# Other homes in SBUF for h^T, the slots and the table of constants of an encoder trunk kernel

## Chip, core and metric

The kernel runs on one core of a Trainium2 chip. The metric is the time of one execution on the device in microseconds, the median of several runs; lower is better.

## What is computed

Two layers of a bidirectional encoder trunk on 512 tokens of width 1024, all in float32. Each layer projects the normed input once (`w_in`, 1024 by 11,168 columns), feeds four token mixers and their gates from it, and merges the branches:

```python
for l in range(DEPTH):                       # 2
    h = rmsnorm(x, norm_pre[l])
    p = split_in(einsum("bsd,de->bse", h, w_in[l]))
    y_a = mixer_a(...) * silu(p["a_g"])      # dilated windows, 18 heads in 3 groups
    y_b = mixer_b(...) * silu(p["b_g"])      # conv and two linear recurrences
    y_c = mixer_c(...) * silu(p["c_g"])      # differential attention, 4 heads
    y_d = mixer_d(...) * silu(p["d_g"])      # latent attention, 6 heads
    g = sigmoid(p["gate"] + b_gate[l])       # 4 x 1024 gates
    merged = sum of g[i] * (y_i @ w_br_i[l]) over the four branches
    x = x + rmsnorm(merged @ w_out[l], norm_post[l])
```

## The kernel before

**Three products for one.** Every dense float32 product is made of three matmuls on operands of type float32r: a matrix is split into a high part (a copy rounded by ScalarE) and a low part (the rest, by VectorE), and `mm3` issues high by high, high by low and low by high into one PSUM bank. So weights come as pairs `wh`, `wl`, the normed and transposed input as `hTh`, `hTl`, a branch's output as `yb0h`, `yb0l` and so on, and the merged activations as `mh`, `ml`. Every matmul loads its stationary operand (128 by 128) anew.

**Which operand stands and which moves.** `item_T` computes 128 output channels at a time: the weights stand, and 512 tokens move, from `hTh`, `hTl` (projections, gates) or from a branch's output (`branch`). `item_tok` and `item_out` compute 128 tokens at a time: the activations stand (a 128-column block of `hTh`, `hTl`, `mh` or `ml`), and 512, 416 or 384 weight columns move. In the rows below the operand ahead of the comma moves and the one behind it stands; `ps<-hTh,wh` has h^T moving, `ps<-wh,hTh` has it standing.

**Where tiles live.** All SBUF is planned by hand. A pool of one-off tiles (`self.cp`) comes first, in `setup`; then 82 slots of 128 by 512 float32 (2048 bytes in each partition), from which nearly every work tile is taken by `slot`; then 4 staging tiles of the same size for raw weights, and small tiles. Tiles are laid one behind another in the order in which the code makes them, each start rounded up to 32 bytes. 1152 bytes of each partition are taken ahead of the first. h^T is two tiles of 8 blocks of 512 float32 (`hTh`, `hTl`, 16,384 bytes each). The table `cst` (9232 bytes: ALiBi distances, rotary tables) is read by VectorE and GpSimd; `junk` is where ScalarE leaves squares whose sums alone are wanted; `ident` is the identity for transposes.

**What sets the order.** A model of the five engines' times (`Sched`) decides, while the program is built, in which order the dense work (`dense_all`), the attention side work (`side_main`) and the recurrence (`side_lru`) are issued. It looks at sizes and tile names, not at addresses. All instructions are recorded from one helper line, L314.

Of the kernel before, what the change touches and what calls it, by code (L numbers as in the profile page):

```python
# [9 lines left out]
F32 = mybir.dt.float32  # L10
# [6 lines left out]
P = 128  # L17
# [17 lines left out]
K_C, K_A1, K_A23, K_RT, K_RN, K_QS, K_END = 0, 896, 1280, 1536, 2048, 2304, 2436  # L35
# [5 lines left out]

N_SLOT = 82
N_STAGE = 4
W_FIRST = 8
BANKS = {"d": 3, "S": 2, "T": 2, "O": 1}
W_MIN = 7
# [316 lines left out]
class Trunk:  # L363
# [131 lines left out]
    def load_w(self, upto):  # L495
        nc = self.nc
        while self.w_dma < min(upto, len(self.specs)):
            src, a, b = self.specs[self.w_dma]
            if self.w_dma < W_FIRST:
                st = self.slot("st")  # L500
            else:
                st = self.stp.tile([P, 512], F32, tag="st", name=self.uid("st"))
                self.clk.take(st, "st", N_STAGE)
            v = st[:, :a * b].rearrange("p (a b) -> p a b", a=a)
# [9 lines left out]
    def pump(self, force=None):  # L514
        cls, self.clk.cls = self.clk.cls, "w"
        self.load_w(max(W_FIRST, self.w_split) + N_STAGE)
        n = 0
        while self.w_split < self.w_dma:
# [10 lines left out]
            del self.stage[i]  # L529
            if i < W_FIRST:  # L530
                self.rel(st)
                if i == W_FIRST - 1:
                    self.done.add("first")
            self.w_split += 1
            n += 1
        self.load_w(max(W_FIRST, self.w_split) + N_STAGE)
        self.clk.cls = cls
# [442 lines left out]
    def side_first(self):  # L980
        V = self.nc.vector
        yield ("n", 2 + 8 + 4 + 8 + W_FIRST)

# [16 lines left out]
        xs.append(self.load_x(self.I["x"], 3))  # L1000
        self.load_w(W_FIRST + N_STAGE)
        self.nc.sync.dma_start(self.cst, self.I["consts"][:, P:])
# [705 lines left out]
    def setup(self):  # L1708
        nc, I = self.nc, self.I
        V, S = nc.vector, nc.scalar  # L1710
        self.cst = self.cp.tile([P, K_END - P], F32, name="cst")
        self.ident = self.cp.tile([P, P], F32, name="ident")
        self.junk = self.cp.tile([P, 512], F32, name="junk")
        self.tiny_t = self.cp.tile([P, 1], F32, name="tiny")
        nc.gpsimd.memset(self.tiny_t, 1.0e-30)
        self.tiny = self.tiny_t[:, 0:1]
        self.eps_t = self.cp.tile([P, 1], F32, name="eps")
        nc.gpsimd.memset(self.eps_t, EPS)
        self.eps = self.eps_t[:, 0:1]
        self.hTh = self.cp.tile([P, 8, 512], F32R, name="hTh")  # L1720
        self.hTl = self.cp.tile([P, 8, 512], F32R, name="hTl")
        self.prm = self.cp.tile([P, 256], F32, name="prm")
        self.prm_h = self.cp.tile([P, P], F32, name="prmh")
        self.prm_d = self.cp.tile([P, 32], F32, name="prmd")
        self.clk.free_of_war = {self.junk.tensor.name}
        self.clk.by_block = {t.tensor.name for t in (self.hTh, self.hTl)}

# [97 lines left out]
    def run(self):  # L1825
# [6 lines left out]
        with tc.tile_pool(name="c", bufs=1) as self.cp, tc.tile_pool(name="s", bufs=N_SLOT) as self.sp, \  # L1832
                tc.tile_pool(name="st", bufs=N_STAGE) as self.stp, tc.tile_pool(name="sm", bufs=40) as self.smp, \
                tc.tile_pool(name="sw", bufs=6) as self.smw, \
# [147 lines left out]
```

## Time and profile before

| | us |
|---|---|
| median of 3 runs (1566.57 to 1566.65) | 1566.58 |
| the profiled execution | 1567.27 |
| its span, first to last instruction | 1565.5 |
| PE (TensorE matmuls) busy in it | 1550.1 (99%) |
| DVE (VectorE) busy | 882.7 (56%) |
| ACT (ScalarE) busy | 734.8 (47%) |
| granted TensorE clock, mean | 0.997 of full speed |

A PE that is busy 99% of the span says that a matmul is always under way, not that matmuls follow one another as fast as they could: they overlap, and the end of one is modelled. How fast they go is read from the starts of two matmuls in the timeline, or of the first and the last of a run, divided by the steps between them. This is called the pace below.

### The profile page before, as it was taken

The numbers are of one execution on the slowest core, as the hardware profiler recorded it, in microseconds if no ns is written. First come the engines' busy times: TensorE is split into PE (matmuls) and PEld (weight loads), VectorE is DVE, ScalarE is ACT, GpSimd is POOL, SyncE is SP. The second block draws the span as 40 slices with busy tenths as digits, with TensorE's granted clock in tenths as the row PEclk, the third lists the DMA queues.
The fourth block names the chain that finished last, engine by engine and source line by source line (L and its number), as shares of the span: only waits on it lengthen the run. The fifth ranks groups of instructions, "written<-read, shape, count | busy, mean of one in ns | idle before, by whom it ended". The sixth has DMA issues, their size and how long they took to land.

```text
span 1565.5 us, 21989 instructions
## 1 busy us (share of the span) xinstructions
PE 1550.1 (99%) x8024; PEld 1257.3 (80%) x8024; DVE 882.7 (56%) x1898; ACT 734.8 (47%) x1626; POOL 59.1 (4%) x254
## 2 busy tenths in 40 slices
PE   8999999999999999999999999999999999999998
PEld 7877888778787888888888878887787787788886
DVE  5698754446544453556657876544546445445553
ACT  5576653343444443443456765434435445334331
POOL 1300000000000100000010000000000001000000
PEclk9999999999999999999999999999999999999999
DMA  6422132223232333253252212232232223332521
GB/s 209 140 58 57 44 101 78 78 71 94 68 79 71 86 74 105 58 174 104 72 166 54 68 55 80 79 85 68 75 94 61 77 72 86 80 95 58 183 71 54
DMA packets 170884, 136.34 MB, mean 87 GB/s; under 512 B 25230, under 2 KB 158360, under 8 KB 170648
## 3 DMA queue, kind: packets, MB, share of 16 engines
q1 hardware_dynamic: 170776, 134.94, 31.1%
q8 instruction: 63, 1.03, 0.3%
q14 instruction: 45, 0.37, 0.1%
HBM read 129.45 MB, written 4.27 MB: 85 GB/s over the span
## 4 chain that ended last, share of the span: by engine, by line
PE 98%; DVE 1%; ACT 1%; DMA 0%; issue 0%; SPq 0%; DVEq 0%; ACTq 0%
PE ps L314 98%; DMA st<-in_w_in 0%; DVE rr L314 0%; SPq L314 0%; DVE hTl L314 0%; ACT hTh L314 0%; DVE rp L314 0%; ACT h L314 0%; DVE x L314 0%; ACT wh L314 0%; DVE wl L314 0%; ACT junk L314 0%; DVE h L314 0%; DVE xc L314 0%; DVE yb2l L314 0%
## 5 line engine op out<-in xcount | busy, mean ns | idle before, releaser
L314 PE MATMUL ps<-hTh,wh 128*128 128x512 f32 x1280 | 520.9, 407 | 0.7 <-DVE ud L314 0.7
L314 PE MATMUL ps<-hTh,wl 128*128 128x512 f32 x1280 | 505.8, 395 | 0.0
L314 PE MATMUL ps<-hTl,wh 128*128 128x512 f32 x1280 | 505.1, 395 | 0.0
L314 DVE TENSOR_TENSOR wl<-st,wh 128x512 fp32r<-128x512 f32 (+2 forms) x464 | 301.7, 666 | 278.5 <-ACT wh L314 276.9
L314 PEld LDWEIGHTS ps<-hTh,wh 128*128 128x128 f32 x1280 | 241.1, 188 | 65.8 <-issue 13.2
L314 PEld LDWEIGHTS ps<-hTh,wl 128*128 128x128 f32 x1280 | 240.9, 188 | 56.4
L314 ACT ACTIVATE wh<-st 128x512 fp32r<-128x512 f32 (+2 forms) x464 | 265.3, 606 | 43.9 <-DMA st<-in_w_in 37.4
L314 PEld LDWEIGHTS ps<-hTl,wh 128*128 128x128 f32 x1280 | 241.6, 189 | 49.2
L314 DVE CUSTOM_DVE_ANT_0 pC<-ps,cst 128x512 f32<-128x512 f32 x64 | 41.6, 688 | 83.4 <-PE ps L314 83.4
L314 PE MATMUL ps<-wh,hTh 128*128 128x416 f32 (+2 forms) x192 | 72.0, 375 | 0.7 <-ACT hTh L314 0.6
L314 PE MATMUL ps<-wl,hTh 128*128 128x416 f32 (+2 forms) x192 | 70.3, 366 | 1.5 <-DVE wl L314 1.5
L314 PE MATMUL ps<-wh,hTl 128*128 128x416 f32 (+2 forms) x192 | 70.3, 366 | 0.2
L314 ACT ACTIVATE pA<-pA,on 128x256 f32<-128x256 f32 x96 | 47.9, 501 | 38.4 <-DVE on L314 38.1
L314 ACT ACTIVATE pD<-ps,mx 128x512 f32<-128x512 f32 x48 | 32.9, 686 | 66.1 <-DVE mx L314 66.0
L314 ACT ACTIVATE pC<-pC,mx 128x512 f32<-128x512 f32 x64 | 45.8, 717 | 36.3 <-DVE mx L314 36.3
L314 DVE CUSTOM_DVE_ANT_0 pA<-ps,cst 128x256 f32<-128x256 f32 x96 | 36.0, 420 | 32.2 <-PE ps L314 32.2
L314 PE MATMUL ps<-wh,mh 128*128 128x512 f32 x128 | 50.0, 391 | 0.0
L314 PE MATMUL ps<-wh,ml 128*128 128x512 f32 x128 | 49.9, 390 | 0.0
L314 PE MATMUL ps<-wl,mh 128*128 128x512 f32 x128 | 49.9, 390 | 0.0
L314 ACT ACTIVATE wtC<-ps 128x512 f32<-128x512 f32 x32 | 19.0, 595 | 52.0 <-PE ps L314 52.0
L314 ACT ACTIVATE junk<-ps,rd 128x128 f32<-128x128 f32 x32 | 11.7, 365 | 65.1 <-DVE oC L314 64.4
L314 DVE TENSOR_REDUCE mx<-ps 128x1 f32<-128x512 f32 x48 | 32.7, 686 | 14.7 <-PE ps L314 14.5
(390 smaller groups left out, 2210.7 us busy)
## 6 DMA issues: line engine op xcount, KB each, us to landing
st<-in_w_in SPq DMA_DIRECT2D x216, 256.0 KB
st<-in_w_in SPq DMA_DIRECT2D x240, 128.0 KB
st<-in_w_out SPq DMA_DIRECT2D x32, 256.0 KB
x<-in_x SPq DMA_DIRECT2D x16, 256.0 KB
st<-in_w_br_c SPq DMA_DIRECT2D x16, 256.0 KB
x<-x SPq DMA_DIRECT2D x16, 256.0 KB
st<-in_w_in SPq DMA_DIRECT2D x16, 208.0 KB
st<-in_w_in SPq DMA_DIRECT2D x16, 192.0 KB
```

The costliest lines, as they stand in the source:

```text
L314: op.fn(*op.a, **op.k)
```

## The change

Nothing is computed otherwise: every engine gets the same instructions in the same order, with the same waits. Other is where tiles live. `ident`, the two one-column tiles and `prm_d` come first, and a pad of 48 float32; then h^T; then `junk`, `prm` and `prm_h`; then `cst` and a pad of 120 float32; then the slots. The pads are tiles that nothing reads or writes.

```diff
+PAD = (48, 120)
...
-        self.cst = self.cp.tile([P, K_END - P], F32, name="cst")
+
         self.ident = self.cp.tile([P, P], F32, name="ident")
-        self.junk = self.cp.tile([P, 512], F32, name="junk")
         self.tiny_t = self.cp.tile([P, 1], F32, name="tiny")
...
         self.eps = self.eps_t[:, 0:1]
+        self.prm_d = self.cp.tile([P, 32], F32, name="prmd")
+        self.cp.tile([P, PAD[0]], F32, name="pad0")
         self.hTh = self.cp.tile([P, 8, 512], F32R, name="hTh")
         self.hTl = self.cp.tile([P, 8, 512], F32R, name="hTl")
+        self.junk = self.cp.tile([P, 512], F32, name="junk")
         self.prm = self.cp.tile([P, 256], F32, name="prm")
         self.prm_h = self.cp.tile([P, P], F32, name="prmh")
-        self.prm_d = self.cp.tile([P, 32], F32, name="prmd")
+        self.cst = self.cp.tile([P, K_END - P], F32, name="cst")
+        self.cp.tile([P, PAD[1]], F32, name="pad1")
```

The homes that follow, in bytes from the start of a partition:

| tile | before | its remainder by 512 | now | its remainder by 512 |
|---|---|---|---|---|
| `hTh` (8 blocks of 2048) | 13024 | 224 | 2048 | 0 |
| `hTl` | 29408 | 224 | 18432 | 0 |
| the slots (82 of 2048), then 4 staging tiles | 47456 on | 352 | 48128 on | 0 |
| `ident` | 10400 | 160 | 1152 | 128 |
| `junk` | 10912 | 160 | 34816 | 0 |
| `cst` | 1152 | 128 | 38400 | 0 |

A matmul operand begins at its tile's start, or 512, 1024 or 1536 bytes behind it. So before, every operand out of h^T begins at remainder 224 by 512, and every other operand of a dense matmul at 352; now all of them at 0.

## Rows read from the trace of the kernel before

**Rows 1.** The page: busy time of engines and share of span.
```profile
PE 1550.1 (99%) x8024; PEld 1257.3 (80%) x8024; DVE 882.7 (56%) x1898; ACT 734.8 (47%) x1626; POOL 59.1 (4%) x254
```

**Rows 2.** The chain that ended last: its longest pieces; start us, us, what.
```profile
92.64 703.92 PE ps L314 x3683
...
959.24 599.30 PE ps L314 x3131
```

**Rows 3.** Groups of PE, by shape: names, shapes, xcount, busy us, mean ns.
```profile
L314 PE MATMUL ps<-hTh,wh 128*128 128x512 f32 x1280 | 520.9, 407 | 0.7 <-DVE ud L314 0.7
L314 PE MATMUL ps<-hTh,wl 128*128 128x512 f32 x1280 | 505.8, 395 | 0.0
L314 PE MATMUL ps<-hTl,wh 128*128 128x512 f32 x1280 | 505.1, 395 | 0.0
L314 PE MATMUL ps<-wh,mh 128*128 128x512 f32 x128 | 50.0, 391 | 0.0
...
L314 PE MATMUL ps<-wh,hTh 128*128 128x512 f32 x64 | 25.8, 402 | 0.0
L314 PE MATMUL ps<-wh,hTl 128*128 128x512 f32 x64 | 25.2, 394 | 0.0
L314 PE MATMUL ps<-wl,hTh 128*128 128x512 f32 x64 | 25.2, 394 | 0.0
```

**Rows 4.** Timeline of PE, layer 2, first and last of 144 h^T matmuls.
```profile
1372.00 0.39 PE L314 MATMUL ps<-hTh,wh 128*128 128x512 f32 x1
...
1405.36 0.40 PE L314 MATMUL ps<-hTh,wl 128*128 128x512 f32 x1
```

**Rows 5.** Timeline of PE, end of layer 1, first and last of 132 slot matmuls.
```profile
732.95 0.39 PE L314 MATMUL ps<-ya0h,wh 128*128 128x512 f32 x1
...
762.66 0.39 PE L314 MATMUL ps<-wh,ml 128*128 128x512 f32 x1
```

**Rows 6.** Timeline of PE, early in layer 1, first and last of 102 h^T matmuls.
```profile
36.97 0.40 PE L314 MATMUL ps<-hTh,wh 128*128 128x512 f32 x1
...
60.44 0.39 PE L314 MATMUL ps<-hTh,wl 128*128 128x512 f32 x1
```

**Rows 7.** Those three stretches: busy us of each engine (instructions), PE clock, DMA share, GB/s.
```profile
1371.99:1405.37 33.38, 33.38 (x145) 26.86 (x143) 11.31 (x21) 8.93 (x16) 0.00 (x0) 1.00 0.34 96
732.94:762.67 29.73, 29.73 (x133) 24.61 (x132) 18.91 (x38) 12.13 (x25) 0.00 (x0) 1.00 0.26 82
36.96:60.45 23.49, 23.49 (x103) 19.06 (x103) 12.04 (x26) 11.36 (x23) 15.35 (x59) 1.00 0.72 211
```

**Rows 8.** Timeline of PE, a short slot run of branch c, first and last of 24.
```profile
547.17 0.39 PE L314 MATMUL ps<-yc0h,wh 128*128 128x512 f32 x1
...
552.43 0.40 PE L314 MATMUL ps<-yc3h,wl 128*128 128x512 f32 x1
```

**Rows 9.** Timeline of PE, branch b, nine slot matmuls behind four transposes.
```profile
249.20 0.60 PE L314 MATMUL ps<-ident,pD 128*128 128x128 f32 x4
249.55 0.48 PE L314 MATMUL ps<-yb0h,wh 128*128 128x512 f32 x1
249.87 0.40 PE L314 MATMUL ps<-yb0l,wh 128*128 128x512 f32 x1
250.10 0.39 PE L314 MATMUL ps<-yb0h,wl 128*128 128x512 f32 x1
250.33 0.39 PE L314 MATMUL ps<-yb1h,wh 128*128 128x512 f32 x1
...
251.46 0.39 PE L314 MATMUL ps<-yb2h,wl 128*128 128x512 f32 x1
```

**Rows 10.** Timeline of PE, slot matmuls of 384 columns, six from 71.62 on, then h^T.
```profile
71.62 0.34 PE L314 MATMUL ps<-ukvh,cTh 128*128 128x384 f32 x1
...
72.66 0.40 PE L314 MATMUL ps<-hTh,wh 128*128 128x512 f32 x1
```

## The prediction

> **What bounds the kernel.** I read the page's busy times first: PE has 1550.1 us of the span, DVE 882.7, ACT 734.8 [rows 1]. The chain that ended last says that this is a bound and not only a long row of work: one of its pieces is 3683 PE instructions over 703.92 us and another 3131 over 599.30 us, without a step to any other engine [rows 2]. So the time is the number of matmuls times the pace at which they start, and what a change does to DVE, ACT or DMA counts only if it makes PE wait. Most matmuls are of one kind: 3840 with h^T moving and 512 columns, in three groups of 1280, and 192 with h^T standing [rows 3].
>
> Next I read the pace from the starts. In a run of 144 matmuls with h^T, the first starts at 1372.00 and the last at 1405.36 us: 33.36 us over 143 steps, 233.3 ns each [rows 4]. In a run of 132 that begins in branch a and ends in `w_out`, where both operands lie in slots, it is 29.71 us over 131 steps, 226.8 ns [rows 5]. The shape is the same (512 columns, 128 by 128 standing), and so is the granted clock, 1.00 [rows 7], which is the level of 2.4 GHz. The h^T run is 6.5 ns slower per matmul.
>
> Who is to blame? Not the neighbours: in the slower run DVE worked 11.31 of 33.38 us (34%) and ACT 8.93 (27%), in the faster one 18.91 of 29.73 (64%) and 12.13 (41%) [rows 7]. Not the DMA: in an early run of 102 h^T matmuls its share was 0.72 instead of 0.34, and the pace was 23.47 us over 101 steps, 232.4 ns [rows 6, 7]. Not a wait: each run is one unbroken PE sequence. What is left is where the operands lie. An h^T operand begins at remainder 224 by 512 bytes, a slot operand at 352; in rows 4 the two kinds meet in each matmul, in rows 5 both operands begin at 352. The change takes that difference away.
>
> A second thing in the pace concerns all of them. Six slot matmuls of 384 columns take 1.04 us, 173.3 ns each [rows 10]. Between 384 and 512 columns lie 226.8 - 173.3 = 53.5 ns, 0.418 ns per column; 512 columns are then 214.0 ns, and 12.8 ns per matmul are left that don't depend on its length. What these are the trace doesn't say.
>
> **The change part by part.** No instruction is removed, added or moved, and no queue gets other work. The two pads cost nothing: nothing touches them.
>
> *h^T against slots.* The upper end of the gain is the whole difference of the long runs, 6.5 ns [rows 4, 5]. But a slot run begins slowly too. Behind transposes, the steps from 249.87 to 250.33 are 230 ns each, and only then, from 250.33 to 251.46, does it go on at 226 ns [rows 9]; a run of 24 in branch c took 5.26 us over 23 steps, 228.7 ns [rows 8], 4.6 ns under the long h^T run. Much of the dense work is cut into shorter pieces than that by side work, so I take 4 ns for all 3840 + 192 matmuls [rows 3]: **4032 x 4.0 ns = 16.1 us**. The lower end is 1 ns (a third of the first steps' advantage, since at 230 ns they are some 3 ns under the h^T pace), 4 us; the upper one 6.5 ns, 26.2 us.
>
> *Slots against slots.* Their remainder goes from 352 to 0, but that of the one operand against the other stays 0. I take no gain. The bounds are all of the 12.8 ns that don't depend on the length, for 4032 h^T matmuls and the 1008 slot matmuls of 512 columns in the branch and output products (13 x 8 x 3 x 2 and 8 x 4 x 2 x 3 x 2, together 1008): 64.5 us; and on the other side what the second rival says.
>
> *The other matmuls.* 8024 [rows 1] less 4032 and 1008 leaves some 3000: transposes, attention products of 64 to 128 columns, and a few hundred of 384 or 416. No row has one of these kinds at two homes; I take nothing. As bounds serve the 6.5 ns per 512 columns of rows 4 and 5, that is 1.6 ns per 128 columns, either way: 4.8 us more or less.
>
> *`cst`, `junk`, `ident`, parameters.* Their readers and writers are DVE, ACT and GpSimd, which have 44% of the span and more to spare [rows 1]; PE covers what they might gain or lose. If that cover were gone, PE would show waits for them within these long chains, and it shows none [rows 2]. DMA lands in slots at other remainders; at a share of 0.26 to 0.72 in the stretches looked at [rows 7] it has room as well.
>
> *What is late next.* Nothing, at 16 us: PE stays the bound, with its weights split ahead of it as before.
>
> *The sum.* The profiled execution took 1567.27 us (span 1565.5), 0.69 above the median of 1566.58. 1567.27 - 16.1 = 1551.2; against the median, **1550.5 us**, 1.0% faster.
>
> **The rivals.** First, *the constant part goes too*. If some of the 12.8 ns is paid because operands begin in the middle of what the array fetches at a time, a start at 0 saves it for every matmul. For it speaks that the cost doesn't grow with the length; against it, that nothing in this trace begins at a rounder place than another and goes faster. In full this is 64.5 us on top of up to 26.2: 1566.6 - 90.7 = 1476; half of it on top of 16 gives 1518. The page "TensorE: Matmul & The Clock Gate" of the Trainium skill (Back-to-back issue gap) gives the columns over the clock and about 2.5 ns for the step between warm matmuls, about 216 ns for 512 columns; the settled slot run at 226.8 ns [rows 5] doesn't agree, and by that page an estimate of 11 ns per matmul, 55 us, could still go.
>
> Second, *the place itself is bad, and the difference is not what counts*. Say that a beginning at a multiple of 512 costs as much as h^T's 224 does now. Then the h^T matmuls keep their 233 ns, and the 1008 slot matmuls go from 226.8 to it: 6.5 us more, 1573.1 us. This rival decides against the change once the slot pairs lose more than the h^T ones gain: with h^T unchanged, 3.1 us more (0.2%, about what a measurement of this kernel can tell from no change) need 3.1 ns for each slot matmul; against a gain of 4 ns for h^T, they would have to lose 16 ns. For it speaks that every tile now begins at the same remainder by 1024, so whatever is decided by these address bits happens to all at once; against it, that slots already share one remainder and are the faster kind.
>
> Third, *the change does nothing to PE*: h^T is slower for another reason than its remainder, for instance because it lies low in the partition, and stays so. h^T remains the lowest large tile. Then the time is 1566.6, with 1563.5 to 1569.7 around it. The same page of the Trainium skill (Step-by-step: what each phase is for) says that the array reads moving and standing operands through two ports of their own, so that loading the next weights takes nothing from the running matmul. By that rule how two operands lie to each other could not matter, and the sum would be 0; the trace has two paces that neither clock nor neighbours explain [rows 4, 5, 7], which speaks against the rule as far as it goes.
>
> **How the numbers follow.** The forecast gets 0.47; its own range is 1540 to 1563 us (26.2 and 4 us of gain). The constant part, in full or in part, gets 0.22 (1476 to 1540). No effect gets 0.17, the bad place 0.14 (up to 1573 and beyond). Faster by over 0.2%: 0.47 + 0.22 = 0.69; within 0.2%: 0.17; slower: 0.14. The range takes in the forecast, most of the first rival and most of "no effect", and leaves out the slow rival and the very end of the first: 1480 to 1569.
>
> **What would show it.** Right: in the long run of rows 4, 143 steps in about 32.4 us (226.8 ns), the run of rows 5 still at 226 to 227 ns, the same instruction counts, PE still 98% of the chain. If the first rival holds, both runs come under 224 ns and the slot matmuls of 384 columns under 171. If the second, the run of rows 5 comes to 230 ns or more. If the third, rows 4 stay at 233. I am wrong altogether if the pace improves and the time doesn't: then PE would have to wait for `wl` or `wh`, and steps in the chain to DVE, ACT or DMA would show where.

## The result and the profile after

The changed kernel takes **1548.98 us** (median of 4 runs, 1548.64 to 1550.21) against 1566.62 us for the kernel before (4 runs, 1566.57 to 1567.01): a ratio of 0.9888, 95% interval 0.9871 to 0.9905, 17.6 us less. The prediction was 1550.5 us. The profiled execution took 1549.14 us with a span of 1547.4, 18.1 under the span before.

The page of the changed kernel, busy time of engines and the chain that ended last (to be read beside [rows 1]; the helper line is L315 here, as the edit added a line):

```profile
PE 1532.6 (99%) x8024; PEld 1254.7 (81%) x8024; DVE 882.4 (57%) x1898; ACT 735.3 (48%) x1626; POOL 61.0 (4%) x254
...
PE 96%; DVE 1%; ACT 1%; DMA 0%; issue 0%; SPq 0%; DVEq 0%; ACTq 0%
```

The same number of instructions on every engine; DVE, ACT and the weight loads are busy as long as before, within 3 us. PE alone lost 17.5 us, and is still 99% of the span. Its share of the chain is 96% instead of 98, so some steps to ACT and DVE are now on it where I had expected none; they don't show as lost time, since PE's idle time in the span was 15.4 us and is 14.8 (span less busy). Its groups, by shape (beside [rows 3]; the last column but one is the mean duration in ns, whose end is modelled):

```profile
L315 PE MATMUL ps<-hTh,wh 128*128 128x512 f32 x1280 | 515.8, 403 | 1.1 <-DVE ud L315 1.1
L315 PE MATMUL ps<-hTl,wh 128*128 128x512 f32 x1280 | 499.7, 390 | 0.0
L315 PE MATMUL ps<-hTh,wl 128*128 128x512 f32 x1280 | 499.5, 390 | 0.0
L315 PE MATMUL ps<-wh,mh 128*128 128x512 f32 x128 | 50.0, 390 | 0.0
```

The h^T groups fell from 395 to 390 ns (407 to 403 for `ps<-hTh,wh`, the first of each three), and stand where the groups of `w_out` stood already. Those didn't move.

Now the pace, from the timeline of PE: first and last matmul of the long h^T run (144), of the slot run (132), of the early h^T run (102) and of the short slot run (24), in the order of [rows 4], [rows 5], [rows 6], [rows 8]:

```profile
1356.35 0.39 PE L315 MATMUL ps<-hTh,wh 128*128 128x512 f32 x1
...
1388.76 0.39 PE L315 MATMUL ps<-hTh,wl 128*128 128x512 f32 x1
...
723.72 0.39 PE L315 MATMUL ps<-ya0h,wh 128*128 128x512 f32 x1
...
753.42 0.39 PE L315 MATMUL ps<-wh,ml 128*128 128x512 f32 x1
...
36.63 0.39 PE L315 MATMUL ps<-hTh,wh 128*128 128x512 f32 x1
...
59.55 0.39 PE L315 MATMUL ps<-hTh,wl 128*128 128x512 f32 x1
...
540.59 0.39 PE L315 MATMUL ps<-yc0h,wh 128*128 128x512 f32 x1
...
545.83 0.39 PE L315 MATMUL ps<-yc3h,wl 128*128 128x512 f32 x1
```

| run | steps | before, ns per step | after |
|---|---|---|---|
| long h^T run | 143 | 33.36 / 143 = 233.3 | 32.41 / 143 = 226.6 |
| slot run | 131 | 29.71 / 131 = 226.8 | 29.70 / 131 = 226.7 |
| early h^T run | 101 | 23.47 / 101 = 232.4 | 22.92 / 101 = 226.9 |
| short slot run | 23 | 5.26 / 23 = 228.7 | 5.24 / 23 = 227.8 |

h^T matmuls now go at the pace of slot matmuls. What the other engines did in the two long stretches, and the granted clock, is as in [rows 7]:

```profile
1356.34:1388.77 32.43, 32.43 (x145) 26.84 (x143) 11.23 (x20) 8.94 (x16) 0.00 (x0) 1.00 0.34 98
723.71:753.43 29.72, 29.72 (x133) 24.60 (x132) 18.91 (x38) 12.13 (x25) 0.00 (x0) 1.00 0.25 82
```

**Where the 18.1 us of the span came from.** Adding the steps from each matmul's start to the next start, over the whole trace: behind the 3840 matmuls with h^T moving 914.5 us became 897.9 (16.6 less); behind the 192 of 512 columns with h^T standing, 45.2 became 44.4 (0.8); behind the matmuls of the same shape with two slot operands (1169 steps), 271.1 became 270.4 (0.7). That is all of it: the other steps, transposes and attention products among them, come to the same sum before and after, within 0.1 us.

### The profile page after: what moved, and what is told of

Its sections match the earlier page's. It is cut to its first block, busy times and chain, and to the rows that moved or that the text cites. A ratio compares the mean times of both kernels' runs of the same rounds, so it can differ in the third digit from the quotient of the medians.

```text
span 1547.4 us, 21989 instructions
## 1 busy us (share of the span) xinstructions
PE 1532.6 (99%) x8024; PEld 1254.7 (81%) x8024; DVE 882.4 (57%) x1898; ACT 735.3 (48%) x1626; POOL 61.0 (4%) x254
## 4 chain that ended last, share of the span: by engine, by line
PE 96%; DVE 1%; ACT 1%; DMA 0%; issue 0%; SPq 0%; DVEq 0%; ACTq 0%
PE ps L315 96%; DMA st<-in_w_in 0%; ACT lg L315 0%; DVE wl L315 0%; DVE lg L315 0%; DVE hTl L315 0%; ACT hTh L315 0%; ACT wh L315 0%; DVE rr L315 0%; SPq L315 0%; DVE rp L315 0%; ACT h L315 0%; ACT L315 0%; DVE x L315 0%; ACT la L315 0%
## 5 line engine op out<-in xcount | busy, mean ns | idle before, releaser
L315 PE MATMUL ps<-hTh,wh 128*128 128x512 f32 x1280 | 515.8, 403 | 1.1 <-DVE ud L315 1.1
L315 PE MATMUL ps<-hTl,wh 128*128 128x512 f32 x1280 | 499.7, 390 | 0.0
L315 PE MATMUL ps<-hTh,wl 128*128 128x512 f32 x1280 | 499.5, 390 | 0.0
L315 DVE TENSOR_TENSOR wl<-st,wh 128x512 fp32r<-128x512 f32 (+2 forms) x464 | 301.6, 666 | 272.0 <-ACT wh L315 271.1
L315 PEld LDWEIGHTS ps<-hTh,wh 128*128 128x128 f32 x1280 | 240.4, 188 | 62.8 <-issue 12.8
L315 ACT ACTIVATE wh<-st 128x512 fp32r<-128x512 f32 (+2 forms) x464 | 265.5, 606 | 42.2 <-DMA st<-in_w_in 35.9
L315 PEld LDWEIGHTS ps<-hTh,wl 128*128 128x128 f32 x1280 | 240.3, 188 | 52.2
L315 PEld LDWEIGHTS ps<-hTl,wh 128*128 128x128 f32 x1280 | 240.8, 188 | 44.5
L315 DVE CUSTOM_DVE_ANT_0 pC<-ps,cst 128x512 f32<-128x512 f32 x64 | 41.6, 689 | 81.5 <-PE ps L315 81.5
L315 PE MATMUL ps<-wh,hTh 128*128 128x416 f32 (+2 forms) x192 | 71.6, 373 | 0.6 <-ACT hTh L315 0.6
L315 PE MATMUL ps<-wl,hTh 128*128 128x416 f32 (+2 forms) x192 | 70.2, 365 | 1.7 <-DVE wl L315 1.6
L315 PE MATMUL ps<-wh,hTl 128*128 128x416 f32 (+2 forms) x192 | 69.9, 364 | 0.1
L315 ACT ACTIVATE pA<-pA,on 128x256 f32<-128x256 f32 x96 | 47.9, 501 | 38.1 <-DVE on L315 37.9
L315 ACT ACTIVATE pD<-ps,mx 128x512 f32<-128x512 f32 x48 | 33.0, 687 | 65.9 <-DVE mx L315 65.7
L315 ACT ACTIVATE pC<-pC,mx 128x512 f32<-128x512 f32 x64 | 45.8, 717 | 36.2 <-DVE mx L315 36.2
L315 DVE CUSTOM_DVE_ANT_0 pA<-ps,cst 128x256 f32<-128x256 f32 x96 | 36.0, 420 | 31.5 <-PE ps L315 31.4
L315 PE MATMUL ps<-wh,mh 128*128 128x512 f32 x128 | 50.0, 390 | 0.0
L315 PE MATMUL ps<-wh,ml 128*128 128x512 f32 x128 | 49.8, 389 | 0.0
L315 PE MATMUL ps<-wl,mh 128*128 128x512 f32 x128 | 49.8, 389 | 0.0
L315 ACT ACTIVATE wtC<-ps 128x512 f32<-128x512 f32 x32 | 19.1, 596 | 50.5 <-PE ps L315 50.5
L315 ACT ACTIVATE junk<-ps,rd 128x128 f32<-128x128 f32 x32 | 11.7, 365 | 63.8 <-DVE oC L315 63.1
L315 PEld LDWEIGHTS ps<-wl,hTh 128*128 128x128 f32 x192 | 36.6, 191 | 5.9 <-DVE wl L315 2.8
```

Of the source, the lines that this page charges most:

```text
L315: op.fn(*op.a, **op.k)
```

## The experiments

Theory D (the one of the prediction) says that the distance between the beginnings of the two operands decides. Theory P says that h^T's own place at a multiple of 512 does, theory O that it is the order of the tiles (h^T lower, the table behind it).

### The old order, with equal remainders

In the kernel before, two pads alone:

```diff
+        self.cp.tile([P, 32], F32, name="pad0")
         self.hTh = self.cp.tile([P, 8, 512], F32R, name="hTh")
...
         self.prm_d = self.cp.tile([P, 32], F32, name="prmd")
+        self.cp.tile([P, 96], F32, name="pad1")
```

> The order of tiles is that of the kernel before (the table of constants first, junk ahead of h^T); two pads alone are added, so that h^T and the slots both begin at remainder 352 by 512 bytes: equal to each other, but not at 0. If the difference between the moving and the standing operand decides (my theory), the time is that of the change, 1547 to 1551 us, and the long h^T runs go at about 227 ns. If a beginning at a multiple of 512 is what helps, h^T at 352 gains only what 352 is better than 224 by itself, and slots gain nothing: between 1551 and 1567 us, long runs between 228 and 233 ns. If the new order of tiles (h^T lower, constants behind it) is what helps, nothing changes: 1566 to 1567 us, 233 ns.

It took 1549.54 us, ratio 0.9884 (0.9867 to 0.99). The long h^T run in its timeline:

```profile
1355.99 0.39 PE L314 MATMUL ps<-hTh,wh 128*128 128x512 f32 x1
...
1388.40 0.39 PE L314 MATMUL ps<-hTh,wl 128*128 128x512 f32 x1
```

32.41 us over 143 steps, 226.6 ns: the whole gain, with the tiles in their old order and nothing at a multiple of 512. Theories O and P fall; 512 bytes of pads in the kernel before would have done.

### Slots at 128, h^T at 0

```diff
-PAD = (48, 120)
+PAD = (48, 24)
```

> The changed kernel with a smaller second pad: h^T stays at remainder 0 by 512, the slots go to 128, so that slots lie 128 behind h^T, as in the kernel before (352 against 224). If the difference decides, the gain goes away in full: 1564 to 1569 us, long h^T runs at 232 to 233.5 ns, slot runs still at 226.8. If h^T's own beginning at 0 helps, h^T runs stay at 227 to 228 ns and the time is 1548 to 1552 us.

1566.92 us, ratio 0.9997 (0.9988 to 1.0006): the gain is gone, though h^T begins at 0. The long h^T run:

```profile
1374.40 0.40 PE L315 MATMUL ps<-hTh,wh 128*128 128x512 f32 x1
...
1407.77 0.40 PE L315 MATMUL ps<-hTh,wl 128*128 128x512 f32 x1
```

33.37 us over 143 steps, 233.4 ns, as before.

### Slots at 256 and at 32

```diff
-PAD = (48, 120)
+PAD = (48, 56)
...
+PAD = (48, 128)
```

The first of these sizes puts the slots at 256, the second at 32.

> h^T at 0, slots at 256 by 512. If the difference decides and repeats each 256 bytes, this is the change again, 1547 to 1551 us and 227 ns; if it repeats each 512 or more, h^T runs are slower than 230 ns and the time is 1558 us or more. If h^T's own beginning decides: 1547 to 1551 us.

> h^T at 0, slots at 32 by 512 bytes. If the difference decides in steps coarser than 32 bytes, or if h^T's own beginning decides, it is the change again, 1547 to 1551 us. If any difference costs the same, 1564 to 1569 us and h^T runs at 233 ns. If slots that begin at an odd multiple of 32 pay for it themselves, slot runs go over 228 ns.

At 256: 1548.99 us, ratio 0.988 (0.986 to 0.99). So slots 256 bytes further cost nothing, as a pattern that repeats each 256 bytes has it; 512 or 1024 have no part in it. At 32: 1568.34 us, ratio 1.0008 (0.9997 to 1.0018), no gain left. The long h^T run at 256, 143 steps in 32.42 us (226.7 ns):

```profile
1356.13 0.39 PE L315 MATMUL ps<-hTh,wh 128*128 128x512 f32 x1
...
1388.55 0.39 PE L315 MATMUL ps<-hTh,wl 128*128 128x512 f32 x1
```

and at 32, in 33.37 us (233.4 ns):

```profile
1371.57 0.40 PE L315 MATMUL ps<-hTh,wh 128*128 128x512 f32 x1
...
1404.94 0.40 PE L315 MATMUL ps<-hTh,wl 128*128 128x512 f32 x1
```

That an operand begins at an odd multiple of 32 costs the slot matmuls nothing here: their run of 131 steps keeps 226.9 ns.

```profile
731.67 0.39 PE L315 MATMUL ps<-ya0h,wh 128*128 128x512 f32 x1
...
761.39 0.39 PE L315 MATMUL ps<-wh,ml 128*128 128x512 f32 x1
```

### Slots at 64, 192, 224

```diff
-PAD = (48, 120)
+PAD = (48, 8)
...
+PAD = (48, 40)
...
+PAD = (48, 48)
```

In this order they put the slots at 64, 192 and 224.

> h^T at 0, slots at 64 by 512. The differences 0 and 256 gave 1549 us, 32 and 128 some 1567 to 1568. If only whole multiples of 256 are good, 1564 to 1569 us and h^T runs at 232 to 233 ns; if the order is by some other power of two, 1549 us. A run under 226 ns would show that the constant 12.8 ns depends on the difference as well, and that there is a better layout than the change; I expect none.

> h^T at 0, slots at 192 by 512, that is 64 short of 256. If only whole multiples of 256 are good, 1564 to 1569 us, h^T runs at 232 to 233 ns. If the sign of the difference matters (the standing operand behind or ahead of the moving one), this and the run at 64 differ by over 3 us.

> h^T at 0, slots at 224 by 512, 32 short of 256, the nearest miss from the other side than the run at 32. If only whole multiples of 256 are good, 1564 to 1569 us. If misses in this direction are harmless, 1549 to 1552 us.

64: 1568.05 us, ratio 1.0014 (1.0003 to 1.0024). 224: 1568.22 us, 1.0012 (1.0002 to 1.0023). But 192: **1556.26 us, 0.9938 (0.9918 to 0.9958)**, over half of the gain, which theory D as I had put it ("whole multiples of 256 alone") didn't expect. The kernel has a control for it: besides the matmuls where h^T moves and a slot stands, there are those where a slot moves and h^T stands, so each layout tries two distances of opposite sign. With slots at 192, the long run with h^T moving (first two rows) and a run of 24 with h^T standing:

```profile
1362.15 0.40 PE L315 MATMUL ps<-hTh,wh 128*128 128x512 f32 x1
...
1394.89 0.40 PE L315 MATMUL ps<-hTh,wl 128*128 128x512 f32 x1
...
98.23 0.40 PE L315 MATMUL ps<-wh,hTh 128*128 128x512 f32 x1
...
103.60 0.40 PE L315 MATMUL ps<-wh,hTl 128*128 128x512 f32 x1
```

32.74 us over 143 steps is 229.0 ns; 5.37 us over 23 is 233.5. With slots at 64, the same two runs:

```profile
1371.61 0.39 PE L315 MATMUL ps<-hTh,wh 128*128 128x512 f32 x1
...
1404.98 0.40 PE L315 MATMUL ps<-hTh,wl 128*128 128x512 f32 x1
...
97.70 0.39 PE L315 MATMUL ps<-wh,hTh 128*128 128x512 f32 x1
...
102.97 0.39 PE L315 MATMUL ps<-wh,hTl 128*128 128x512 f32 x1
```

33.37 us over 143 is 233.4 ns; 5.27 us over 23 is 229.1. The two have changed places. So the distance has a sign: what counts is how far the standing operand begins behind the moving one, by 256 bytes, and at 192 some two thirds of the price are gone (229.0 between 233.3 and 226.7), whichever of the two is h^T.

### h^T's low part alone at 128

```diff
-PAD = (48, 120)
+PAD = (48, 88)
...
+        self.cp.tile([P, 32], F32, name="pad2")
         self.hTl = self.cp.tile([P, 8, 512], F32R, name="hTl")
```

> The changed kernel with h^T's low part alone moved, by 32 float32, to remainder 128; its high part and the slots stay at 0. One third of the h^T matmuls (1280 of 3840, every third one) have the low part moving. If a mismatch costs only the matmul that has it, a third of the gain is lost: 1554 to 1556 us. If one mismatch disturbs the next matmuls too (the slot runs took several steps to settle behind a transpose), two thirds or more are lost: 1560 to 1567 us. If the mismatch counts only where two neighbours share it, 1549 us.

1559.09 us, ratio 0.9957 (0.9941 to 0.9974). The kernel before took 1566.17 us on that chip, so 7.1 of 17.6 us of gain are left and some 60% is lost, between what I had put for the two cases. The timeline shows both. In the long run the matmul that has the mismatch pays, and it alone; the columns are start, duration, names:

```profile
1380.14 0.39 PE L315 MATMUL ps<-hTh,wh 128*128 128x512 f32 x1
1380.37 0.40 PE L315 MATMUL ps<-hTl,wh 128*128 128x512 f32 x1
1380.60 0.39 PE L315 MATMUL ps<-hTh,wl 128*128 128x512 f32 x1
1380.83 0.39 PE L315 MATMUL ps<-hTh,wh 128*128 128x512 f32 x1
1381.05 0.40 PE L315 MATMUL ps<-hTl,wh 128*128 128x512 f32 x1
1381.29 0.39 PE L315 MATMUL ps<-hTh,wl 128*128 128x512 f32 x1
```

From an `hTl` to the next start it is 0.23 or 0.24 us, from the others 0.22 or 0.23; in nanoseconds a settled stretch near the end of this run reads 234, 226, 227, 234, 226, 226. The whole run has 228.9 per step, a third of 6.6 over 226.7. But the early run of 102 goes at 233.3 ns (34.87 to 58.44 us, 101 steps), and there all three kinds are slow: 236, 234 and 230 ns, over and over. Of the 19 h^T runs of 25 or more steps in this trace, ten go at 229 ns, six at 231 and three at 233. Why one mismatch in three is contained in one place and spreads in another, these runs don't show.

The same run tries the standing operand and the one that is loaded meanwhile apart, where h^T stands: `wl` moving with `hTh` standing are at distance 0, while `hTl`, 128 off, is loaded for the next matmul; then `hTl` stands, and `hTh` is loaded.

```profile
866.37 0.40 PE L315 MATMUL ps<-wl,hTh 128*128 128x512 f32 x1
866.38 0.19 PEld L315 LDWEIGHTS ps<-wh,hTl 128*128 128x128 f32 x1
...
866.61 0.40 PE L315 MATMUL ps<-wh,hTl 128*128 128x512 f32 x1
866.61 0.19 PEld L315 LDWEIGHTS ps<-wh,hTh 128*128 128x128 f32 x1
...
866.84 0.39 PE L315 MATMUL ps<-wh,hTh 128*128 128x512 f32 x1
```

Both steps pay. Take the 186 steps of 512 columns that wait for no late weight load (those under 260 ns; in the changed kernel the next load begins 3 ns behind the matmul's own start in them, as the median, and over 80 ns behind in each longer one). On average it is 232.1 ns behind `wl,hTh` and 233.8 behind `wh,hTl`, against 227.9 and 228.2 in the change; behind `wh,hTh`, where both are at 0, it is 228.8 against 228.2. So a step is slow when the operand loaded meanwhile is misplaced, though the running pair is not, and the step behind it is slow too. Every settled stretch of this kind reads 227, 232 or 233, 234 over and over; that its middle step is slow by the load, and not by a spreading as in the early run, is likely by this, but not shown apart.

### Slots at 96

```diff
-PAD = (48, 120)
+PAD = (48, 16)
```

> h^T at 0, slots at 96 by 512. By the runs so far the distance of the standing operand behind the moving one, by 256 bytes, sets the pace: 0 gives 228 ns on average, 32, 64, 128 and 224 give 232.5 to 233.5, 192 gives 229.7 (and 230.0 where slots move and h^T stands). Here h^T moving has distance 96, and h^T standing has 160. If the cheap side begins behind 128, the 186 matmuls with h^T standing go at 229 to 231 ns and those with h^T moving at 233; if 192 alone is half good, both go at 233. The time is 1564 to 1569 us either way.

One run: 1571.69 us beside 1566.46 to 1568.16 for the kernel before, a little over what I expected. With h^T moving (distance 96) it is 234.0 ns on average, the dearest of all; with h^T standing (distance 160) 233.5. So 192 alone is partly good.

All distances, as means over the steps under 260 ns; 3612 steps with h^T moving, 186 with h^T standing:

| standing begins behind moving by (mod 256) | h^T moves, ns | h^T stands, ns |
|---|---|---|
| 0 | 228.1 | 228.1 |
| 32 | 233.1 | 232.9 |
| 64 | 233.3 | 233.4 |
| 96 | 234.0 | not run |
| 128 | 232.6 | 232.5 |
| 160 | not run | 233.5 |
| 192 | 229.7 | 230.0 |
| 224 | 233.2 | 233.0 |

The two columns come from different matmuls, and save at 0 and 128 from different layouts; they agree within 0.3 ns.

### The identity at 256, and the change again

The transposes' moving operand at remainder 0 by 256 like everything else, and beside it the changed kernel itself on the same chip:

```diff
-PAD = (48, 120)
+PAD = (32, 120)
...
-        self.ident = self.cp.tile([P, P], F32, name="ident")
...
+        self.cp.tile([P, 16], F32, name="padi")
+        self.ident = self.cp.tile([P, P], F32, name="ident")
         self.prm_d = self.cp.tile([P, 32], F32, name="prmd")
```

> The changed kernel with the identity for the transposes at remainder 256 by 512 (0 by 256) instead of 128; all else where it was. If float32 transposes pay for a distance like the float32r matmuls do, some 690 of them gain up to 1 ns each: 1548.3 us or a little less, and a step between two transposes goes from 109 to 108 ns. If they don't, 1549 us, within 0.3 us of the change.

> The changed kernel again, on the chip of the run with the identity moved: 1548.5 to 1550.5 us, ratio 0.988 to 0.990 to the kernel before.

1549.29 us (ratio 0.9886, 0.9871 to 0.99) and 1549.77 us (0.9887, 0.9871 to 0.9904): no difference that the intervals can tell. The step from one transpose to the next, without waits, is 108.8 ns on average in both layouts. Float32 transposes pay nothing for a distance of 128, so there is no better layout in this direction.

### Half of the standing columns

```diff
-                            self.mm3(ps, ah, al, hi[:, 0, :], lo[:, 0, :], k == 0, k == 7)
+                            if 0 < k < 7:
+                                self.mm3(ps[:64], ah[:, :64], al[:, :64], hi[:, 0, :], lo[:, 0, :], False, False)
+                            else:
+                                self.mm3(ps, ah, al, hi[:, 0, :], lo[:, 0, :], k == 0, k == 7)
```

> In the output product, the matmuls of six of the eight row blocks load 64 of the 128 standing columns and make half of the outputs, so that part of the sum is left out for the other half of the tokens. This asks what the 12.8 ns are that don't depend on the columns moved. If they are the load of the standing operand taking time from the moving one, they halve with it: these matmuls follow one another at 220 ns instead of 226.7. If they are a fixed cost of a switch, 226 to 227 ns as before.

The time of one run, 1549.21 us, is that of the change. Three matmuls with a half load in the output product, and three with a full one behind them:

```profile
746.05 0.39 PE L315 MATMUL ps<-wh,mh 128*64 128x512 f32 x1
746.27 0.40 PE L315 MATMUL ps<-wl,mh 128*64 128x512 f32 x1
746.51 0.39 PE L315 MATMUL ps<-wh,ml 128*64 128x512 f32 x1
746.74 0.39 PE L315 MATMUL ps<-wh,mh 128*128 128x512 f32 x1
746.97 0.39 PE L315 MATMUL ps<-wl,mh 128*128 128x512 f32 x1
747.19 0.39 PE L315 MATMUL ps<-wh,ml 128*128 128x512 f32 x1
```

The loads themselves are shorter in the trace, 134 ns instead of 188:

```profile
L315 PEld LDWEIGHTS ps<-wh,mh 128*64 128x64 f32 x96 | 12.9, 134 | 8.3
...
L315 PEld LDWEIGHTS ps<-wh,mh 128*128 128x128 f32 x32 | 6.0, 188 | 2.2
```

The steps are not: 230 ns on average over 287 of them, unevenly (mostly 224 to 236), against 226.7 for full ones in the change. So the part of a step that doesn't grow with the columns moved did not shrink with the load's length; what it is stays open.

## Why the prediction was right, point by point

**The bound and the suspect were right.** PE's starts set the time, and the difference between two paces that neither clock nor neighbours explained [rows 4, 5, 7] was one of homes in SBUF. The old order with two pads, and slots at 128 with h^T at 0, show that it is the distance between the two operands, not the order and not the place.

**The main term was right in size.** I took 4.0 ns for each of 4032 matmuls, 16.1 us, between 6.5 in long runs and some steps of settling [rows 8, 9]. Measured: (914.5 - 897.9 + 45.2 - 44.4) / 4032 = 4.3 ns, 17.4 us. The long runs gave all of the 6.5 (233.3 to 226.6), and the shorter ones less, for the reason that I had given. Before, an undisturbed step with h^T moving takes 232.1 to 232.9 ns wherever in its run it stands; in the changed kernel it takes 231.1 as one of the first three, 228.6 up to the ninth, 227.1 up to the 21st and 226.8 further on. So the start of a run gains 1 ns and the rest of a long one 6. That their mean would be 4 ns was a guess between two bounds, and it came out close. The 0.7 us of the slot matmuls I had not counted. Their mean over steps under 260 ns fell from 228.3 to 227.6 ns, and it is the h^T matmuls ahead of them that do it: the first three slot steps behind h^T took 231.9 ns before, 227.2 in the change, 227.1 with the old order and equal remainders, and 232.0 with slots at 128, while from the tenth on they take 226.7 in all four.

**The first rival is refuted.** Nothing further went when operands began at a round place: 226.7 ns at remainder 0 and at 352 alike. Its price rested on little. I had the 12.8 ns from six matmuls of 384 columns in 1.04 us [rows 10]; in the changed kernel the same six take 1.07 us (70.63 to 71.70), so a run that short is not settled. The size itself holds, though: the 384-column matmuls with h^T standing go at 174 ns there, as the median of 178 steps, close to the 173.3 that I had taken. A beginning at 0 saves none of it, and half of the standing columns didn't halve it. It cost me only width: the range went down to 1480 for it.

**The second rival, a bad place,** is refuted by slots at 352, at 32 or at 0: the slot run keeps 226.7 to 226.9 ns in all of them. **The third, no effect,** fell with the result. It went with a rule of the page "TensorE: Matmul & The Clock Gate" of the Trainium skill (Step-by-step: what each phase is for), by which loading the next weights takes nothing from the running matmul. Here two float32r operands go at 226.7 or 233.3 ns by their distance alone; and with h^T's low part alone at 128, a step whose own pair is at distance 0 went from 227.9 to 232.1 ns while a misplaced operand was loaded. The measurement decides here, and it speaks against the rule for this type. As the step behind it is slow too, and a mismatch was seen to spread, how much of the price falls on the load and how much on the operand that stands is open.

**The other matmuls and the rest, at nothing,** were right, as the steps above show, but two readings behind them were off. The attention products, to which I gave 64 to 128 columns, move 128 to 512, and 162 of the matmuls that I counted there have the very shape of the slot matmuls. And `ident` is read by TensorE itself, as the transposes of [rows 9] show, not by the other engines alone; that its new home costs and gains nothing is what the run with the identity at 256 and the steps of the transposes show, and does not follow from my reason.

**What I missed** is that the distance has a sign and a partly good value. It did not touch the number, since the change makes all distances 0.

## What to carry to other kernels

Where TensorE is the bound, busy time hides the pace: divide a run's first-to-last start by its steps, once for each kind of operand pair, and ask why two kinds of one shape differ. For float32r matmuls of 512 columns with a fresh standing operand each, let moving and standing operands begin at the same remainder by 256 bytes; here two small pads (512 bytes of each partition in the old order) were worth 1.1%, and neither larger alignment nor the order of tiles added anything. Shorter matmuls gave less in the same change: with h^T standing, undisturbed steps of 384 columns went from 176.0 to 174.5 ns, and those of 416 stayed (188.1 and 188.2).

## What the runs showed that I had not expected

The settled paces are sharp: in the long h^T run of 143 steps 226.7 ns at distance 0, 233.3 to 234.3 at 32, 64, 96, 128 and 224, and 229.0 at 192. A bad distance upsets matmuls with a good one behind it in one place and not in another (the low part at 128: 236, 234 and 230 ns in the early run, 234 and 226 side by side in the late one). Where h^T stands, one misplaced operand of three is paid for twice, in the step that loads it and in the step in which it stands. And a standing operand of 64 columns, loaded in 134 instead of 188 ns, made steps 3 to 4 ns longer, not shorter.
